# Down projection of a gated ConvFFN: eight of eleven pairs of K tiles as seven products of quarters, with the weights' sums added up in DRAM

## The chip, the cores and the metric

The kernel runs on one core of one Trainium2 chip. The metric is the device time in microseconds (us) of one execution. The engines are TensorE (PE: matmuls; PEld: its weight loads), VectorE (DVE), ScalarE (ACT), GpSimd (POOL) and SyncE (SP), which here only issues DMAs. Each engine works through its own queue in order and waits on semaphores; DMA transfers run on 16 DMA engines that all queues share.

## The reference

One layer of a decoder with 512 positions and a width of 1024: a norm, one wide input projection, a short convolution branch, a gated delta rule branch, a merge, an output projection, and then the part that the change touches:

```python
def conv_ffn(h, w_up, conv_w, w_down):
    up = causal_dwconv(h @ w_up, conv_w)
    gate, val = jnp.split(up, [D_FF], axis=-1)      # D_FF = 2816
    return (jax.nn.silu(gate) * val) @ w_down       # (512, 2816) @ (2816, 1024)

x = x + conv_ffn(rmsnorm(x, norm_ffn_g), w_up, ffn_conv_w, w_down)
return rmsnorm(x, norm_final_g)
```

All of it is in float32, with inputs in float32.

## The kernel before

**Matmuls.** Every large product is done in three matmuls: each operand is split into a high part and the rest (names `wh`, `wl` for weights, `as`, `ts`, `us`, `h` for activations), and low x high, high x low and high x high are added in PSUM. All these matmuls come from one helper, `mm` (L107 before, L108 after). PSUM has 8 banks of 128x512, which `bank()` hands out in turn.

**Jobs.** The program is a list of jobs. A job is a block of weights of 1 MB (four quarters of 128x512, tile `raw`, two buffers) and a function that multiplies with it. `run_jobs` walks the list: it finishes the splitting of this job's block, queues the splitting of the next one, issues the load of the block two jobs on (SP queue), and then emits the job's matmuls. Splitting a quarter is one ACT cast (`wh`, L139 before, L140 after) and one DVE subtraction (`wl`, L140 before, L141 after); twelve `wh` and twelve `wl` quarters are held, three jobs of four.

**What is emitted between matmuls.** `mm` counts columns, and after every 2048 of them calls `tick`, which advances queues of small tasks (splits, evacuations of PSUM, chains of the delta rule) by a step. This, and a scheduler that follows the program's order and its own estimates, sets the order in each engine's queue.

**Projections already in seven products.** Most blocks of the input and up projections already use seven products of quarters instead of eight (`sum_job`): DVE adds weight quarters in SBUF, in `raw` (L160 before), ahead of the split, and 128x256 matmuls follow.

**The down projection.** 2816 rows of `w_down` are 22 K tiles, 11 pairs (11 jobs, from `row_jobs`). The activation is the stationary operand and the weight the moving one. Per pair, `part(g, t)` does, for each of the 4 tiles of 128 positions, 2 halves of the output width and 2 K tiles, three matmuls of 128x512: 48 per pair, 528 in all, into 8 PSUM banks that accumulate over all 11 pairs. `split_ffn` (ACT L298, DVE L299) splits the activation of two K tiles per job. The last two jobs are interleaved by position tiles, so that `fin2(t)` (residual add, final norm, store: DVE L1253 and on, one POOL power L1259, DMAs) starts as soon as tile t is done.

**POOL** has work in the delta rule, four small powers after the output projection (`fin1`, L1142) and four at the end (`fin2`, L1259), and issues no DMA.

Of the kernel before, what the change touches and what calls it, by code (L numbers as in the profile page):

```python
# [9 lines left out]
F32 = mybir.dt.float32  # L10
# [6 lines left out]
P = 128  # L17
# [42 lines left out]
def layer_kernel(ctx, tc, x, norm_mix_g, w_in, w_ab, conv_a_w, gdn_conv_w, gdn_A_log, gdn_dt_bias,  # L60
# [18 lines left out]
    def bank():  # L79
        return ps.tile([P, 512], F32, tag="ps", name=nm("ps"))  # L80


    chains, mids, backs, evacs, splits, sums_of = (deque() for _ in range(6))
    nmm = [0]

    def advance(queue, n):
        while n and queue:
            queue[0].step()
            if queue[0].done:
                queue.popleft()  # L90
            else:
                n -= 1

    def tick():
        advance(backs, 1)
        advance(mids, 1)
        advance(chains, 1)
        advance(evacs, 2)
        advance(splits, 1)
        advance(sums_of, 1)  # L100

    def drain(queue):
        while queue:
            advance(queue, 1)
# [19 lines left out]
    class Block:  # L124
        def __init__(self, src, quarter=(4, P)):
            self.src, self.quarter = src, quarter
            self.raw, self.ready = None, False
# [24 lines left out]
    class SumBlock(Block):  # L152
        def split(self):
# [25 lines left out]
            self.part("12", r[1])  # L179
            yield  # L180

    def run_jobs(jobs):
        jobs[1][0].load()
        for i, (block, use) in enumerate(jobs):
            Task(block.split()).finish()
            drain(splits)
            if i + 1 < len(jobs):
                splits.append(Task(jobs[i + 1][0].split()))
            if i + 2 < len(jobs):
                jobs[i + 2][0].load()  # L190
            use(block.wh, block.wl)


# [20 lines left out]
    def activation_sums(x_, ts, xf):  # L214


        for k in range(0, ND, 2):
            dve.tensor_tensor(out=xf[:, k:k + 2], in0=x_[0][:, k:k + 2].bitcast(F32),
                              in1=x_[1][:, k:k + 2].bitcast(F32), op=ALU.add)
            yield  # L220
            yield
        b = [[xf[:, K * 4:K * 4 + 4, T * HS:T * HS + HS] for T in range(2)] for K in range(2)]

        def to(i, dst, a, c):
            dve.tensor_tensor(out=dst, in0=a, in1=c, op=ALU.subtract)
            yield
            act.copy(out=ts[0][:, i], in_=dst)
# [715 lines left out]
    st = {}  # L943
    held = {}

    def open_conv():
# [172 lines left out]
    def open_o():  # L1119
        drain(evacs)  # L1120
        p1.close()
        fp = ctx.enter_context(tc.tile_pool(name="fp", bufs=1))
        st["x1"] = fp.tile([P, NT, D], F32, name="x1")
        st["h2"] = [fp.tile([P, ND, S], F32R, name=f"h2{i}") for i in range(2)]
# [66 lines left out]
    def split_ffn(k):  # L1191
        if "as" not in st:
            st["as"] = [st["up"].tile([P, 8, S], F32R, tag=f"t{i}", name=f"as{i}") for i in range(2)]
        split(st["as"], k % 8, ffn(k))

    def gate_c(g):
        def c(j, o):
            m = 2 * g + j
            t = st["cvp"].tile([P, S], F32, tag="g", bufs=4, name=nm("g"))
            yield from conv(t, o, ff_w(m), 3)  # L1200
            act.activation(out=t, in_=t, func=AF.Silu)
            gates[m] = t
            yield
        return c
# [29 lines left out]
        sums_of.append(Task(activation_sums(h2, st["ts"], xf)))  # L1234

    for g in range(NF // 2):
        def up_job(i, c, plain):
            if plain:
                return col_job(w_up, i, lambda: st["h2"], c)
            return sum_job(w_up, i, lambda: st["h2"], hsums, c, pair_out)  # L1240

        gj = up_job(g, gate_c(g), g < 2 or g == NF // 2 - 1)
        vj = up_job(NF // 2 + g, val_c(g), True)
        jobs += [(gj[0], first_gate), (vj[0], first_val)] if g == 0 else [gj, vj]

    def fin2(t, acc):
        cvp, x1 = st["cvp"], st["x1"]
# [14 lines left out]
        for sl in halves:  # L1262
            nc.sync.dma_start(out=out2[t * P:(t + 1) * P, sl], in_=y[:, sl])

    def ahead(g):
        for kk in range(2):
            split_ffn(2 * g + kk)
            yield

    def open_down():  # L1270
        drain(evacs)
        Task(ahead(0)).finish()

    def down_x(g):
        return [e[:, 2 * g % 8:2 * g % 8 + 2] for e in st["as"]]
# [56 lines left out]
```

## Time and profile before

| | |
|---|---|
| time, median of 3 runs | 985.68 us (985.62 to 985.8) |
| the profiled execution's own time | 985.69 us |
| its span, first to last instruction | 984.0 us |
| granted TensorE clock, mean | 0.999 |
| PE busy | 974.1 us (99%) |
| DVE busy | 678.8 us (69%) |
| ACT busy | 470.0 us (48%) |
| POOL busy | 60.2 us (6%) |
| DMA | 97.71 MB, 99 GB/s over the span |

Times in the views are from the span's start. "Busy" of PE is the time in which any matmul is under way; matmuls overlap, so their own durations (0.39 us) are longer than the distance from one to the next, and it is the distance that counts. The profile names tiles by the program's names with the numbers left out.

### The profile page before, as it was taken

The page shows a single profiled execution, that of the slowest core. Times are in us where ns is not written, and L with a number is a line of the kernel's source. Part 1 is how long each engine was busy: PE and PEld are TensorE (multiplying, and loading weights), DVE is VectorE, ACT ScalarE, POOL GpSimd, SP SyncE. Part 2 cuts the span into 40 slices and gives each one's busy share as a digit, 9 for nine tenths or more (in the row PEclk, how much of TensorE's full clock was granted, in tenths as well). Part 3 has the DMA queues.
Part 4 walks back from the last instruction along what each step waited for, and adds up shares of the span by engine and source line. Part 5 has one row for each costly group of instructions (what it writes and reads, how often), then busy time and mean ns, then how long its engine had stood idle before and what let it go on. Part 6 is the DMA issues. An engine that isn't in the chain of part 4 may idle for free.

```text
span 984.0 us, 15795 instructions
## 1 busy us (share of the span) xinstructions
PE 974.1 (99%) x6250; PEld 842.3 (86%) x6250; DVE 678.8 (69%) x1312; ACT 470.0 (48%) x1023; POOL 60.2 (6%) x101
## 2 busy tenths in 40 slices
PE   8999999999999999999999999999999999999997
PEld 6888887888888889999988888988999888888885
DVE  6868686896626868899744543998888888533315
ACT  7686566575344434354732323464545556322313
POOL 3320300302000000000000000000000000000000
PEclk9999999999999999999999999999999999999999
DMA  6434212231312123222532252313332234232202
GB/s 228 163 120 128 83 52 87 73 94 53 94 45 86 44 95 120 87 87 87 171 121 94 86 196 82 109 43 129 98 117 86 86 100 158 86 127 88 86 1 85
DMA packets 33466, 97.71 MB, mean 99 GB/s; under 512 B 19275, under 2 KB 19696, under 8 KB 23024
## 3 DMA queue, kind: packets, MB, share of 16 engines
q1 hardware_dynamic: 33392, 96.70, 29.6%
q8 instruction: 49, 0.80, 0.3%
q14 instruction: 25, 0.20, 0.1%
HBM read 93.27 MB, written 3.42 MB: 98 GB/s over the span
## 4 chain that ended last, share of the span: by engine, by line
PE 94%; ACT 3%; DVE 1%; issue 1%; DMA 0%; POOL 0%; SPq 0%; POOLq 0%
PE ps L107 86%; PE ps L609 1%; PE ps L644 1%; PE ps L818 1%; PE ps L838 1%; PE ps L827 0%; ACT Dm L526 0%; PE ps L806 0%; PE ps L805 0%; PE ps L782 0%; PE ps L776 0%; DMA xt<-in_x_dram 0%; PE ps L1154 0%; ACT wh L139 0%; PE ps L720 0%
## 5 line engine op out<-in xcount | busy, mean ns | idle before, releaser
L139 ACT CAST wh<-raw 128x512 fp32r<-128x512 f32 x378 | 222.5, 619 | 287.2 <-PE ps L107 246.9
L140 DVE TENSOR_TENSOR wl<-raw,wh 128x512 fp32r<-128x512 f32 x378 | 253.5, 690 | 144.9 <-ACT wh L139 143.5
L107 PE MATMUL ps<-hT,wh 128*128 128x512 f32 (+1 forms) x1104 | 317.0, 368 | 0.0
L107 PEld LDWEIGHTS ps<-hT,wh 128*128 128x128 f32 x1104 | 196.3, 189 | 28.4
L107 PE MATMUL ps<-hT,wl 128*128 128x512 f32 (+1 forms) x552 | 194.7, 362 | 0.1
L107 PE MATMUL ps<-h,wh 128*128 128x512 f32 (+1 forms) x704 | 177.9, 341 | 0.0
L107 PEld LDWEIGHTS ps<-h,wh 128*128 128x128 f32 x704 | 122.5, 189 | 15.1
L107 PEld LDWEIGHTS ps<-hT,wl 128*128 128x128 f32 x552 | 104.4, 189 | 14.4 <-DVE wl L140 0.5
L107 PE MATMUL ps<-h,wl 128*128 128x512 f32 (+1 forms) x352 | 114.6, 341 | 0.0
L107 PE MATMUL ps<-wh,as 128*128 128x512 f32 x352 | 108.6, 389 | 0.0
L107 PEld LDWEIGHTS ps<-wh,as 128*128 128x128 f32 x352 | 66.1, 188 | 13.7
L107 PEld LDWEIGHTS ps<-h,wl 128*128 128x128 f32 x352 | 66.7, 190 | 7.6
L107 PE MATMUL ps<-wl,as 128*128 128x512 f32 x176 | 68.5, 389 | 0.0
L107 PE MATMUL ps<-ts,wh 128*128 128x256 f32 x320 | 59.2, 283 | 0.0
L305 DVE SCALAR_TENSOR_TENSOR cv<-ps,wA,cv 128x511 f32<-128x511 f32 (+2 forms) x72 | 53.2, 740 | 4.7 <-ACT cv L302 4.5
L107 PEld LDWEIGHTS ps<-ts,wh 128*128 128x128 f32 x320 | 50.6, 192 | 0.0
L160 DVE TENSOR_TENSOR raw<-raw 128x512 f32<-128x512 f32 x72 | 49.3, 685 | 0.9
L107 PE MATMUL ps<-us,wh 128*128 128x256 f32 x256 | 47.4, 283 | 0.0
L107 PEld LDWEIGHTS ps<-us,wh 128*128 128x128 f32 x256 | 40.5, 192 | 0.0
L107 PE MATMUL ps<-wh,mix 128*128 128x512 f32 x128 | 40.2, 391 | 0.0
L107 PE MATMUL ps<-ts,wl 128*128 128x256 f32 x160 | 40.1, 283 | 0.0
L107 PE MATMUL ps<-yas,wh 128*128 128x512 f32 x128 | 39.6, 389 | 0.0
(260 smaller groups left out, 1297.9 us busy)
## 6 DMA issues: line engine op xcount, KB each, us to landing
raw<-in_w_in_dram SPq DMA_DIRECT2D x36, 1024.0 KB, 5.0
raw<-in_w_up_dram SPq DMA_DIRECT2D x22, 1024.0 KB, 4.9
raw<-in_w_down_dram SPq DMA_DIRECT2D x11, 1024.0 KB, 4.9
raw<-in_w_a_out_dram SPq DMA_DIRECT2D x4, 1024.0 KB, 5.0
raw<-in_w_b_out_dram SPq DMA_DIRECT2D x4, 1024.0 KB, 4.9
raw<-in_w_o_dram SPq DMA_DIRECT2D x4, 1024.0 KB, 5.0
Dm<-gtd SPq DMA_DIRECT2D x4, 512.0 KB, 3.9
x<-in_x_dram SPq DMA_DIRECT2D x4, 512.0 KB, 6.7
```

Source lines behind the costliest of these rows:

```text
L107: pe.matmul(o, lhsT=a, rhs=b, start=start, stop=stop, skip_group_check=free)
L139: act.copy(out=wh, in_=src)
L140: dve.tensor_tensor(out=wl, in0=src, in1=wh.bitcast(F32), op=ALU.subtract)
L160: dve.tensor_tensor(out=r[q], in0=a, in1=b, op=op)
L305: dve.scalar_tensor_tensor(out=dst[:, sh:], in0=src[:, :S - sh], scalar=wcol(j), in1=dst[:, sh:], op0=ALU.mult, op1=ALU.add)
L609: pe.transpose(out=o[:, n * P:(n + 1) * P], in_=src[:, n * P:(n + 1) * P], identity=ident)
L644: pe.matmul(o[:, i], lhsT=kqs[:, a, h, 0, sl], rhs=kqs[:, b, h, :, sl], start=a > 0, stop=a + b == 0)
L818: pe.matmul(o[:, 0:P], lhsT=TTf[:, f, :], rhs=rs[h], start=True, stop=True)
L838: pe.matmul(o[:, 0:P], lhsT=A[:, f, :], rhs=vns[h], start=True, stop=True)
```

## The change

Pairs 0, 1, 2, 3, 4, 5, 7 and 8 (`SEVEN`) are done in seven products of quarters; pairs 6, 9 and 10 (`EIGHT`) stay as they were. A quarter of the weight is one K tile by half of the width (W11, W12 of the pair's first K tile, W21, W22 of its second); a quarter of the activation is one K tile by 256 positions.

- **Sums of weights, in DRAM** (`form_down`). For each of the eight pairs four sums are built: V1 = W12 + W11, V3 = W12 + W22, V2 = V1 + W22, V4 = V2 + W21, each as a copy of 256 KB from DRAM to DRAM and an adding transfer of 256 KB on top. These are 64 transfers, 32 of them adding, all issued by POOL. The steps go round the eight pairs, so that an add follows its copy eight or sixteen transfers later. They are emitted from the place where the convolution branch opens (`open_conv`, after the delta rule).
- **Two passes.** Pass A takes the eight pairs with V2, V3, V1 and W11 (24 matmuls each: 4 products, 2 tiles of positions, 3 matmuls) into all 8 banks. Then pair 6 (48 matmuls) starts the output's own banks; at its start `gather` combines the six banks of pass A (2 ACT copies, 8 DVE operations) and adds the results into the residual `x1` (4 DVE operations). Pass B takes the eight pairs again with W21, W22 and V4 (18 matmuls each). Pairs 9 and 10 end it, interleaved by position tiles with `fin2`, as the last two jobs were. The sum is 480 matmuls of 128x512.
- **Sums of activations.** `prep_a` and `prep_b` form them on DVE for two pairs at a time, and `put` splits them (ACT L1302, DVE L1303) into four slots of tile `xs`; `prep_c` splits the plain pairs.
- **Loads.** A pair in pass A loads three sums and one plain quarter (two DMAs, 1 MB together), in pass B two plain quarters and one sum (0.75 MB). From the third down job on the blocks lie in the space of `h2`, the up projection's input (tile `raws`, four blocks), and loads are issued up to four jobs ahead.

```diff
+    SEVEN, EIGHT = (0, 1, 2, 3, 4, 5, 7, 8), (6, 9, 10)
+    down_q = [w_down[g].rearrange("p k (h n) -> p (k h) n", h=2) for g in range(NG)]
+    vsum = {g: dram.tile([P, 4, S], F32, name=f"vs{g}") for g in SEVEN}
+    def form_down():
+        steps = [[(V1, W12, False), (V3, W12, False)], [(V1, W11, True), (V3, W22, True)],
+                 [(V2, None, False)], [(V2, W22, True)], [(V4, None, False)], [(V4, W21, True)]]
+        for step in steps:
+            for g in SEVEN:
+                for to, q, add in step:
+                    src = down_q[g][:, q] if q is not None else vsum[g][:, V1 if to == V2 else V2]
+                    kw = dict(accum_op=ALU.add) if add else {}
+                    tc.keep_in_program_order(pool.dma_start(out=vsum[g][:, to], in_=src, **kw))
+                    yield
+                    yield
...
+        adds.append(Task(form_down()))
...
+    def put(slot, n, i, m, src):
...
+        act.copy(out=xh, in_=src)
+        dve.tensor_tensor(out=xl, in0=src, in1=xh.bitcast(F32), op=ALU.subtract)
+    def prep_a(c):
+        xv, slot = pairs(SEVEN[2 * c], 2), 2 * c % 4
+        d = pair_out().rearrange("p (g t n) -> p g t n", t=2, n=HS)
+        dve.tensor_tensor(out=d, in0=xv[:, :, 0], in1=xv[:, :, :, 1], op=ALU.subtract)
+        dve.tensor_tensor(out=xv[:, :, 0, 1], in0=d[:, :, 1], in1=xv[:, :, 0, 0], op=ALU.subtract)
+        yield
+        put(slot, 2, 0, 2, xv[:, :, 0])
+        yield
+        put(slot, 2, 2, 2, d)
+        yield
+    def times(slot, i, tau, o, wh, wl, start=False, stop=False, free=False):
+        xh, xl = (e[:, slot, i, tau * P:(tau + 1) * P] for e in st["xs"])
+        for k, (a, b) in enumerate(((xl, wh), (xh, wl), (xh, wh))):
+            mm(o, a, b, start and k == 0, stop and k == 2, free)
+    def use_a(p):
+        def use(wh, wl):
...
+            for name, i in (("v2", 1), ("v3", 2), ("v1", 3), ("11", 0)):
+                for tau in range(2):
+                    times(p % 4, i, tau, banks[name][tau], wh[name], wl[name], p == 0, p == N7 - 1)
+    def gather():
...
+            act.copy(out=u, in_=banks["11"][tau])
+            dve.tensor_tensor(out=u, in0=banks["v2"][tau], in1=u, op=ALU.add)
+            dve.tensor_tensor(out=v[:, lo], in0=banks["v3"][tau], in1=u, op=ALU.add)
...
+            dve.tensor_tensor(out=u, in0=o, in1=u, op=ALU.subtract)
+            dve.tensor_tensor(out=v[:, hi], in0=o, in1=v[:, lo], op=ALU.subtract)
...
+            dve.tensor_tensor(out=x1[:, tau, hi], in0=x1[:, tau, hi], in1=us[tau], op=ALU.add)
+            yield
+            dve.tensor_tensor(out=x1[:, tau + 2], in0=x1[:, tau + 2], in1=vs_[tau], op=ALU.add)
...
+    def use_b(p):
...
+            for name, i in (("21", 0), ("22", 2), ("v4", 1)):
+                for tau in range(2):
+                    o = banks["11" if name == "21" else name][tau]
+                    times((p + 2) % 4, i, tau, o, wh[name], wl[name], free=name == "21")
...
-    jobs += row_jobs(w_down, NF, down_x, fin2, open_down, False, lambda g: splits.append(Task(ahead(g + 1))))
+    down = [([(0, 3, vsum[g][:, V2:V1 + 1]), (3, 4, down_q[g][:, W11:W11 + 1])], ("v2", "v3", "v1", "11"), use_a(p))
+            for p, g in enumerate(SEVEN)]
+    eights = [([(0, 4, down_q[g])], range(4), use_c(q)) for q, g in enumerate(EIGHT)]
+    down.append(eights[0])
+    down += [([(0, 2, down_q[g][:, W21:W22 + 1]), (2, 3, vsum[g][:, V4:V4 + 1])], ("21", "22", "v4"), use_b(p))
+             for p, g in enumerate(SEVEN)]
+    down += eights[1:]
+    jobs += [(FormBlock(runs, names, 2 if i < 2 else min(4, i), down_place(i)), use)
+             for i, (runs, names, use) in enumerate(down)]
```

The order of instructions on SP, POOL, ACT, DVE and PE is the same as before up to the last jobs of the up projection, but for POOL's new transfers. Three places differ in a way that matters below.

On POOL, behind the last power of the delta rule (`fac`), before:

```order
L849 TENSOR_TENSOR fac_3256<-fac_3256,nhalf 128x8
L742 COPY TTf<-TT_3435 32x8x32 x4
L849 TENSOR_TENSOR fac_3766<-fac_3766,nhalf 128x8
L1142 TENSOR_TENSOR r_6527<-r_6527,nhalf 128x1
L1142 TENSOR_TENSOR r_6574<-r_6574,nhalf 128x1
```

and now, with each row's waits (`vs` are the sums in DRAM):

```order
L765 COPY TTf<-TT_3443 32x8x32 x3
L872 TENSOR_TENSOR fac_3774<-fac_3774,nhalf 128x8 [waits DVE_49,Pool_49]
L987 DMA vs_368<-in_w_down_dram 128x512 x2
L987 DMA vs_369<-in_w_down_dram 128x512 x2
L987 DMA vs_370<-in_w_down_dram 128x512 x2
L987 DMA vs_371<-in_w_down_dram 128x512 x2
L987 DMA vs_372<-in_w_down_dram 128x512 [waits DMASW0_49]
L987 DMA vs_372<-in_w_down_dram 128x512 [waits DMASW1_49]
```

All 64 issues stand between the last `fac` and the first power of `fin1`; the first eight wait for nothing, and each later one waits for the transfer eight places ahead of it. No other engine's progress is among their waits.

On PE, at the end of pass A (`ps_9125`, `ps_9126` are the two banks of the product with W11, `ps_9501` a bank taken over from V2's product, `raws`-fed `wh_9449` and on are pair 6):

```order
L108 MATMUL ps_9126<-wh_9427,xs_8991 128x512
L108 MATMUL ps_9125<-wh_9449,xs_8992 128x512
L108 MATMUL ps_9125<-wl_9450,xs_8991 128x512
L108 MATMUL ps_9125<-wh_9449,xs_8991 128x512
L108 MATMUL ps_9125<-wh_9465,xs_8992 128x512
L108 MATMUL ps_9125<-wl_9466,xs_8991 128x512
L108 MATMUL ps_9125<-wh_9465,xs_8991 128x512
L108 MATMUL ps_9501<-wh_9457,xs_8992 128x512
```

Pair 6's first matmul adds to a bank that ACT has to copy out first (`gather`); six matmuls later PE needs a bank that DVE has to have read.

The copies stand here in ACT's queue:

```order
L140 CAST wh_9598<-raws_9106 128x512
L140 CAST wh_9617<-raws_9106 128x512
L1360 COPY u_9487<-ps_9125 128x512
L1360 COPY u_9492<-ps_9126 128x512
L1302 CAST xs_8991<-aTa 128x2x512
```

and the last of the operations behind them in DVE's:

```order
L1366 TENSOR_TENSOR u_9492<-ps_9124,u_9492 128x512
L1367 TENSOR_TENSOR o_9493<-ps_9124,o_9493 128x512
L1371 TENSOR_TENSOR x_6375<-x_6375,u_9487 128x512
L1373 TENSOR_TENSOR x_6375<-x_6375,o_9488 128x1024
L1371 TENSOR_TENSOR x_6375<-x_6375,u_9492 128x512
L1373 TENSOR_TENSOR x_6375<-x_6375,o_9493 128x1024
L1303 TENSOR_TENSOR xs_8992<-aTa,xs_8991 128x2x512
```

where before there were only splits:

```order
L140 TENSOR_TENSOR wl_9329<-raw_9252,wh_9328 128x512
L140 TENSOR_TENSOR wl_9337<-raw_9252,wh_9336 128x512
L140 TENSOR_TENSOR wl_9345<-raw_9252,wh_9344 128x512
L299 TENSOR_TENSOR as_9031<-aTa,as_9030 128x512
L140 TENSOR_TENSOR wl_9353<-raw_9252,wh_9352 128x512
L299 TENSOR_TENSOR as_9031<-aTa,as_9030 128x512
```

The last row of the change's piece (`xs` from `aTa`) prepares the activation that pass B's first job multiplies with; it stands behind all twelve operations of `gather`.

More of the change, by code (lines that the diff above doesn't have):

```diff
@@ L80, in bank @@
         return ps.tile([P, 512], F32, tag="ps", name=nm("ps"))
-    chains, mids, backs, evacs, splits, sums_of = (deque() for _ in range(6))
+    chains, mids, backs, evacs, splits, sums_of, adds = (deque() for _ in range(7))
     nmm = [0]
@@ L100, in tick @@
         advance(sums_of, 1)
+        advance(adds, 1)
     def drain(queue):
@@ L126, in __init__ @@
             self.src, self.quarter = src, quarter
-            self.raw, self.ready = None, False
+            self.raw, self.ready, self.lead = None, False, 2
             self.wh, self.wl = {}, {}
@@ L180, in split, with __init__, load @@
             yield
+    class FormBlock(Block):
+        def __init__(self, runs, names, lead, place):
+            super().__init__(None, (S,))
+            self.runs, self.names, self.lead, self.place = runs, names, lead, place
+        def load(self):
+            if self.raw is not None:
+                return
+            self.raw = self.place()
+            for lo, hi, src in self.runs:
+                nc.sync.dma_start(out=self.raw[:, lo:hi], in_=src)
+        def split(self):
+            if self.ready:
+                return
+            self.ready = True
+            for q, name in enumerate(self.names):
+                self.part(name, self.raw[:, q])
+                yield
     def run_jobs(jobs):
@@ L188, in run_jobs @@
                 splits.append(Task(jobs[i + 1][0].split()))
-            if i + 2 < len(jobs):
-                jobs[i + 2][0].load()
+            for j, (later, _) in enumerate(jobs[i + 2:i + 5]):
+                if later.lead >= j + 2:
+                    later.load()
             use(block.wh, block.wl)
@@ L1123, in open_o @@
         st["x1"] = fp.tile([P, NT, D], F32, name="x1")
-        st["h2"] = [fp.tile([P, ND, S], F32R, name=f"h2{i}") for i in range(2)]
+        st["fp"] = fp
+        st["h2"] = [fp.tile([P, ND, S], F32R, tag=f"h2{i}", name=f"h2{i}") for i in range(2)]
         s7 = st["s7"] = p7.enter_context(tc.tile_pool(name="s7", bufs=2))
@@ L1188, in ffn @@
         return st["aT"][1][:, m - NA, :]
[L1191 to L1194, printed above, removed]
     def gate_c(g):
@@ new lines, in use_a @@
+    def use_a(p):
+        def use(wh, wl):
+            if p == 0:
+                drain(evacs)
+                for name in ("v2", "v3", "v1", "11"):
+                    banks[name] = [bank() for _ in range(2)]
+            if p % 2 == 0:
+                splits.append(Task(prep_a(p // 2 + 1) if p < N7 - 2 else prep_c(0)))
+            for name, i in (("v2", 1), ("v3", 2), ("v1", 3), ("11", 0)):
+                for tau in range(2):
+                    times(p % 4, i, tau, banks[name][tau], wh[name], wl[name], p == 0, p == N7 - 1)
+        return use
@@ new lines, in eight, with use_c, use @@
+    def eight(q, t, wh, wl, first=False, last=False):
+        o = banks["out"][t]
+        for hf in range(2):
+            for k in range(2):
+                free = o[hf] in banks["11"]
+                times((0, 2, 3)[q], 2 * k + t // 2, t % 2, o[hf], wh[2 * k + hf], wl[2 * k + hf],
+                      first and k == 0 and not free, last and k == 1, free)
+    kept = []
+    def use_c(q):
+        def use(wh, wl):
+            kept.append((wh, wl))
+            if q == 0:
+                t_ = Task(gather())
+                t_.step()
+                evacs.append(t_)
+                banks["22"], banks["v4"], banks["r"] = ([bank() for _ in range(2)] for _ in range(3))
+                banks["out"] = ([[banks["11"][e], banks["22"][e]] for e in range(2)] +
+                                [[banks["v4"][e], banks["r"][e]] for e in range(2)])
+                splits.append(Task(prep_b(0)))
+                for t in range(NT):
+                    eight(0, t, wh, wl, True)
+            elif q == 1:
+                eight(1, 0, wh, wl)
+            else:
+                for t in range(NT):
+                    if t:
+                        eight(1, t, *kept[1])
+                    eight(2, t, wh, wl, False, True)
+                    fin2(t, banks["out"][t])
+        return use
@@ L1263, in fin2, with down_place, p @@
             nc.sync.dma_start(out=out2[t * P:(t + 1) * P, sl], in_=y[:, sl])
[L1265 to L1275, printed above, removed]
-    jobs += row_jobs(w_down, NF, down_x, fin2, open_down, False, lambda g: splits.append(Task(ahead(g + 1))))
+    def down_place(i):
+        def p():
+            if i < 2:
+                return wp.tile([P, 4, S], F32, tag="raw", bufs=2, name=nm("raw"))
+            if "raws" not in st:
+                st["raws"] = [st["fp"].tile([P, 2, 4, S], F32, tag=f"h2{e}", name=f"raws{e}") for e in range(2)]
+            e = (i - 2) % 4
+            return st["raws"][e // 2][:, e % 2]
+        return p
+    down = [([(0, 3, vsum[g][:, V2:V1 + 1]), (3, 4, down_q[g][:, W11:W11 + 1])], ("v2", "v3", "v1", "11"), use_a(p))
[7 more added lines that the diff above has]
+             for i, (runs, names, use) in enumerate(down)]
     run_jobs(jobs)
```

51 lines of the change are left out of this document (48 added, 3 removed).

## The prediction

> **What bounds the kernel now.** I read the page first: its busy shares, then its chain of waits.
>
> ```profile
> PE 974.1 (99%) x6250; PEld 842.3 (86%) x6250; DVE 678.8 (69%) x1312; ACT 470.0 (48%) x1023; POOL 60.2 (6%) x101
> ...
> PE 94%; ACT 3%; DVE 1%; issue 1%; DMA 0%; POOL 0%; SPq 0%; POOLq 0%
> ```
>
> PE bounds it, so matmuls removed are time removed, as long as PE goes on finding its operands. The view of the split activation (`as`) gives the down projection's extent, and PE's timeline its pace:
>
> ```profile
> L107 PE MATMUL ps<-wh,as x352: 388/389/389, 857.7 to 977.1; 128*128 128x512 f32 x176
> ...
> L107 PE MATMUL ps<-wl,as x176: 389/389/389, 857.9 to 976.9; 128*128 128x512 f32 x176
> ```
>
> ```profile
> 865.63 0.62 PE L107 MATMUL ps<-wh,as 128*128 128x512 f32 x2
> 866.08 0.39 PE L107 MATMUL ps<-wl,as 128*128 128x512 f32 x1
> 866.31 0.62 PE L107 MATMUL ps<-wh,as 128*128 128x512 f32 x2
> ```
>
> 352 + 176 = 528 matmuls start between 857.7 and 977.1: 119.4 / 527 = 0.2266 us from one to the next, and three take 866.31 - 865.63 = 0.68 in the middle too. So there is no gap to win back; only the number of matmuls counts. The windows show the clock and what stands idle beside it:
>
> ```profile
> 820.00:840.00 20.00, 20.00 (x110) 17.43 (x109) 19.04 (x31) 12.69 (x24) 0.00 (x0) 1.00 0.35 116
> 840.00:860.00 20.00, 20.00 (x90) 16.55 (x89) 10.42 (x17) 8.13 (x14) 0.00 (x0) 1.00 0.26 99
> 860.00:880.00 20.00, 20.00 (x90) 16.57 (x89) 6.99 (x12) 5.70 (x10) 0.00 (x0) 1.00 0.30 106
> ```
>
> From left: span, PE, PEld, DVE, ACT, POOL, clock, DMA share, GB/s. At 860 DVE works 7.0 of 20 us and ACT 5.7; ahead of it, at the end of the up projection, DVE has 19.0 of 20.
>
> **Term 1: PE.** A pair had 48 matmuls and has 24 + 18 = 42; eight pairs make 48 fewer, 480 instead of 528. They have the same shape and the same order of operands (low x high, high x low, high x high), so the same distance: 48 x 0.2266 = **10.9 us**.
> The Trainium skill ("TensorE: Matmul & The Clock Gate", section "Back-to-back issue gap") gives about 131 ns as the sustained distance at 512 columns. By that the change would save 48 x 0.131 = 6.3 us; the rows above show 226.6 ns, so the trace disagrees, and I use the trace.
>
> **Term 2: DVE and ACT in the new passes.** Prices, from the groups by shape:
>
> ```profile
> L139 ACT CAST wh<-raw 128x512 fp32r<-128x512 f32 x378 | 222.5, 619 | 287.2 <-PE ps L107 246.9 <-DVE raw L160 36.3 <-DMA raw<-in_w_in_dram 1.3
> L227 ACT CAST ts<-xf 128x1024 fp32r<-128x1024 f32 x4 | 4.2, 1050 | 5.7 <-issue 3.2 <-DVE xf L225 2.5
> L968 ACT COPY o<-ps 128x512 f32<-128x512 f32 x2 | 1.2, 584 | 2.4 <-PE ps L107 2.4
> L140 DVE TENSOR_TENSOR wl<-raw,wh 128x512 fp32r<-128x512 f32 x378 | 253.5, 690 | 144.9 <-ACT wh L139 143.5
> L225 DVE TENSOR_TENSOR xf<-xf 128x1024 f32<-128x1024 f32 x8 | 9.7, 1215 | 0.0
> L1253 DVE TENSOR_TENSOR x<-x,ps 128x512 f32<-128x512 f32 x8 | 5.5, 687 | 17.4 <-PE ps L107 17.4
> ```
>
> Two jobs of pass A are 48 matmuls, 10.9 us. DVE has 8 `wl` (8 x 0.69 = 5.5) and one `prep_a` (three operations on 1024 elements, one on 512: 3 x 1.215 + 0.69 = 4.3): 9.8 us. ACT has 8 x 0.62 + 2 x 1.05 = 7.1. Two jobs of pass B are 36 matmuls, 8.2 us; DVE has 6 x 0.69 + 0.69 + 1.215 + 0.69 = 6.7, ACT 6 x 0.62 + 1.05 + 0.62 = 5.4. So DVE goes from a third to 90% in pass A, but stays below PE, and PE's `wl` are made a job or more ahead: no loss. Beyond that stands part of the `prep_a` work (the subtractions) in the up projection's last jobs, where DVE has these gaps:
>
> ```profile
> 839.04 0.69 DVE L1211 TENSOR_TENSOR aTb<-v,g 128x512 f32<-128x512 f32 x1
> 841.78 0.69 DVE L140 TENSOR_TENSOR wl<-raw,wh 128x512 fp32r<-128x512 f32 x1 [2.04 <-ACT wh L139]
> ...
> 847.22 0.69 DVE L140 TENSOR_TENSOR wl<-raw,wh 128x512 fp32r<-128x512 f32 x1 [2.83 <-ACT wh L139]
> ```
>
> Up to 840 DVE gets six operations on 1024 elements and two on 512 (8.7 us) where eight of 0.69 for `as` stood (5.5): 3.2 us more, which the gaps of 2.0 and 2.8 us take. The down projection still begins at 857.7.
>
> **Term 3: the seam behind pass A.** Pass A ends 192 x 0.2266 = 43.5 us after 857.7, at 901.2. Pair 6's first matmul waits for ACT's copy of the bank with W11. Three matmuls (0.68 us) follow that bank's last; a matmul's result is out 0.39 - 0.23 = 0.16 us after the next begins, and the copy takes 0.58: 0.74 against 0.68, and a signal each way. I take **0.3 us**; the bounds are nothing, and 0.7 if ACT is a cast late. Six matmuls on (1.4 us) PE needs a bank that DVE reads 0.69 after the copy: in time. Behind it DVE has eight operations on PSUM (8 x 0.69), two adds on 512 and two on 1024 (3.8), then the `xs` operation (1.2) for pass B: 10.5 us from the copy's end, against pair 6's 48 matmuls, 10.9, which start about then. Half a microsecond is spare: nothing lost, but this is the tightest place.
>
> **Term 4: loads.**
>
> ```profile
> GB/s 74 422 29 0 0 41 315 176 0 0 0 168 356 0 0 0 66 348 111 0 8 0 225 299 0 0 0 66 406 53 0 0 4 295 238 0 0 0 0 0
> ...
> raw<-in_w_down_dram SPq DMA_DIRECT2D x7, 1024.0 KB, 4.9
> ```
>
> That is 860 to 940 in slices of 2 us: 1 MB flows in about 3 us, lands 4.9 us after its issue, and then the queue rests. Pass A asks for 1 MB per 5.4 us, pass B for 0.75 MB per 4.1: twice as much as before, a little over half of what is shown. The third block can start only when the up projection has read `h2` for the last time, at 857.7; with 0.75 MB of another block ahead of it in SP's queue that is 1.75 MB at 3 us each and 2 us to land, 865; ACT and DVE split its four quarters by 868.2, and its job begins 10.9 us after 857.7, at 868.6, and needs the last quarter 4 us later. In time.
>
> **Term 5: POOL's 64 transfers.** POOL's timeline has room for them:
>
> ```profile
> 307.69 1.64 POOL L849 TENSOR_TENSOR fac<-fac,nhalf 128x8 f32<-128x8 f32 x1 [28.49 <-DVE fac L848]
> 608.30 0.55 POOL L1142 TENSOR_TENSOR r<-r,nhalf 128x1 f32<-128x1 f32 x1 [298.97 <-DVE r L1141]
> ```
>
> They wait only for each other, so they run in one burst from 309.3. Behind them in POOL's queue stands `fin1`'s power, at 608.3: 298.97 / 64 = 4.67 us each are free, and the first sum is loaded past 820. No row shows a transfer within DRAM or an adding one. The lower bound is 256 KB at the 422 GB/s above, 0.6 us (40 us in all), the upper the 4.9 us of a whole MB, and eight are in flight. I take 1 to 2 us each. Their bytes also pass the loads of 309 to 430 on the same DMA engines; ACT waited for a load 1.3 us in the whole input projection, so a load that takes 8 instead of 5 us is mostly covered. **0**, with 1 us as the upper bound.
>
> **The sum.** 984.0 - 10.9 + 0.3 = 973.4 us of span. The profiled execution took 985.69 with a span of 984.0, 1.7 us around it, and the median is 985.68, so nothing is to be corrected: 973.4 + 1.7 = **975.1 us**. PE had no gap in this stage, so below 985.7 - 10.9 = 974.8 there is nothing to gain but the measurement's own spread.
>
> **Rivals.**
>
> *DVE becomes the bound in pass A.* Were its operations on the strided slots of `xs` and on 256-element pieces a fifth longer, two jobs would take 11.8 us against PE's 10.9: 4 x 0.9 = 3.5 us, 978.6. From 11% on it decides. Against it: the same kind of operation on 1024 elements has 1.215 us in all its rows. A miss at the seam (DVE late for pass B) has this size too.
>
> *POOL's issues hold up DVE: slower.* DVE does get slower beside POOL:
>
> ```profile
> 56.45 1.27 DVE L140 TENSOR_TENSOR wl<-raw,wh 128x512 fp32r<-128x512 f32 x1 [1.89 <-ACT wh L139]
> 56.09 1.09 POOL L518 TENSOR_SCALAR_AFFINE_SELECT Dm<-Dm 128x1024 f32<-128x1024 f32 x1
> ...
> sum 123.00, PE 123.00 PEld 110.92 DVE 96.28 ACT 48.12 POOL 1.64; mean PE 20.50 PEld 18.49 DVE 16.05 ACT 8.02 POOL 0.27
> ```
>
> A `wl` of 0.69 us took 1.27, until POOL's operation was over. The last row is 307 to 430 us, where the transfers run: DVE has 123 - 96.3 = 26.7 us free. If each issue held DVE for over 26.7 / 64 = 0.42 us, DVE would be the bound; from 0.58 us the gain is gone; with POOL's 1.09 us it is 64 x 1.09 - 26.7 = 43 us lost, 1018. Against it: an issue moves no tile through POOL.
> The Trainium skill ("SBUF — State Buffer", section "SBUF: two separate sides") describes this port shared by DVE and GpSimd as an exclusive lock, and says that descriptors of GpSimd's DMAs are written through it; no run here shows yet what an issue holds.
>
> *The transfers are slow.* Over 4.67 us each, `fin1` waits for POOL: at the 6.7 us that 512 KB of `x` take to land, 64 x 6.7 - 299 = 130 us, about 1105. With eight in flight this needs 37 us for one.
>
> *The change does not do what it says*: the distance between matmuls grows as their number falls, 985.7. PE's rows give no reason.
>
> **How the numbers follow.** Forecast 975.1: 0.76. DVE-bound passes (978.6): 0.09. The skill's distance (979.7): 0.02. POOL against DVE: 0.08, of it 0.01 still faster, 0.04 even, 0.03 slower. Slow transfers: 0.03. No effect: 0.02. A measurement here tells 0.2% (2 us) from no change: faster 0.76 + 0.09 + 0.02 + 0.01 = 0.88, same 0.04 + 0.02 = 0.06, slower 0.03 + 0.03 = 0.06. The range takes in the first three: from 974.8 less a little spread, 974.4, to 979.7 and the upper bounds of the seam, 980.5.
>
> **What would show it.** Right: `xs` matmuls from 857.7 to about 966.5, 0.2266 apart; one idle time of PE below 0.7 us near 901; POOL's transfers over well before 608; `wl` still 0.69 us between 309 and 430; the tail behind the last matmul still 6.9 us. Wrong: gaps of PE at each pair of jobs in 857 to 901 (DVE), `wl` over 1 us beside POOL's issues, or `ps` matmuls waiting past 912 for `xs`.

## The result and the profile after

| | before | changed |
|---|---|---|
| time, median | 985.74 us of 4 runs (985.62 to 986.17) | 976.32 us of 4 runs (975.77 to 977.62) |
| ratio, 95% interval | | 0.9906, 0.9888 to 0.9923 |
| profiled execution: time, span | 985.69, 984.0 us | 975.77, 973.7 us |
| spans of its runs | 983.5 to 984.3 us (the 15 beside the first four experiments) | 973.7, 974.0, 974.5, 975.5 us |
| time around the span | 1.68 to 1.76 us (the same 15) | 2.02 to 2.12 us |

The change takes 9.4 us off; 10.6 were forecast. The profiled execution is the fastest of its four.

The head of the page after and its chain of waits:

```profile
PE 963.9 (99%) x6202; PEld 833.4 (86%) x6202; DVE 717.8 (74%) x1360; ACT 490.9 (50%) x1049; POOL 104.1 (11%) x165
...
PE 94%; ACT 2%; DVE 1%; DMA 1%; issue 1%; SPq 0%; POOL 0%; POOLq 0%; ACTq 0%
```

PE has 48 matmuls fewer (6250 to 6202) and still bounds the kernel. The view of the split activation `xs` (durations in ns, first and last start in us):

```profile
L108 PE MATMUL ps<-wh,xs x320: 387/389/504, 857.7 to 966.6; 128*128 128x512 f32 x160
L108 PE MATMUL ps<-wl,xs x160: 389/389/402, 857.9 to 966.4; 128*128 128x512 f32 x160
```

480 matmuls start between 857.7 and 966.6, where 528 did up to 977.1. The last start is 10.5 us earlier: 48 x 0.2266 = 10.9, less 0.3 to 0.4 at the seam. The timeline of PE's weight loads shows that wait, for ACT's copy of a bank with W11:

```profile
901.38 0.19 PEld L108 LDWEIGHTS ps<-wh,xs 128*128 128x128 f32 x1 [0.42 <-ACT u L1360]
```

The windows of the new passes (span, PE, PEld, DVE, ACT, POOL, clock, DMA share, GB/s):

```profile
840.00:860.00 20.00, 20.00 (x90) 16.54 (x89) 16.30 (x23) 7.03 (x11) 0.00 (x0) 1.00 0.15 51
860.00:880.00 20.00, 20.00 (x90) 16.57 (x89) 15.44 (x24) 13.49 (x23) 0.00 (x0) 1.00 0.95 341
880.00:900.00 20.00, 20.00 (x90) 16.57 (x89) 13.99 (x22) 11.53 (x19) 0.00 (x0) 1.00 0.56 176
```

At 860 DVE works 15.4 of 20 us where it worked 7.0, and PE stays full. The windows of POOL's burst, after:

```profile
330.00:350.00 20.00, 20.00 (x90) 16.53 (x90) 13.90 (x20) 7.12 (x12) 7.39 (x9) 1.00 0.93 190
350.00:370.00 20.00, 20.00 (x129) 18.30 (x128) 12.81 (x21) 6.95 (x13) 6.78 (x10) 1.00 1.02 209
390.00:410.00 20.00, 20.00 (x126) 18.11 (x126) 16.00 (x27) 7.85 (x15) 8.20 (x13) 1.00 1.04 278
```

and two of the same before:

```profile
330.00:350.00 20.00, 20.00 (x90) 16.54 (x89) 13.92 (x20) 7.13 (x12) 0.00 (x0) 1.00 0.26 94
350.00:370.00 20.00, 20.00 (x129) 18.30 (x128) 12.80 (x21) 6.95 (x13) 0.00 (x0) 1.00 0.28 94
```

PE and DVE do in them what they did before. What changed is the DMA share: 0.26 to 0.93 and more. The 16 engines are full at 190 to 278 GB/s, loads included, though at 860 loads alone reach 341 GB/s at 0.95. The first issue and the last of the 64, and the power of `fin1` behind them, on POOL's timeline:

```profile
309.29 2.90 POOL L987 DMA_DIRECT2D vs<-in_w_down_dram  x5
...
417.21 0.82 POOL L987 DMA_DIRECT2D vs<-in_w_down_dram  x1 [1.67 <-issue]
608.32 0.57 POOL L1189 TENSOR_TENSOR r<-r,nhalf 128x1 f32<-128x1 f32 x1 [190.29 <-DVE r L1188]
```

So the 64 issues stand within 109 us, 1.7 us each, and POOL then rests for 190 us.

The profiled execution thus does what the sum said. Left to explain are the other runs, up to 1.8 us longer, and 0.35 us more around the span.

### The profile page after: what moved, and what is told of

Its sections match the earlier page's. It is cut to its first block, busy times and chain, and to the rows that moved or that the text cites. A ratio compares the mean times of both kernels' runs of the same rounds, so it can differ in the third digit from the quotient of the medians.

```text
span 973.7 us, 15945 instructions
## 1 busy us (share of the span) xinstructions
PE 963.9 (99%) x6202; PEld 833.4 (86%) x6202; DVE 717.8 (74%) x1360; ACT 490.9 (50%) x1049; POOL 104.1 (11%) x165
## 4 chain that ended last, share of the span: by engine, by line
PE 94%; ACT 2%; DVE 1%; DMA 1%; issue 1%; SPq 0%; POOL 0%; POOLq 0%; ACTq 0%
PE ps L108 86%; PE ps L632 1%; PE ps L667 1%; DMA xt<-in_x_dram 1%; PE ps L841 1%; PE ps L861 1%; PE ps L850 0%; ACT Dm L549 0%; PE ps L829 0%; PE ps L828 0%; PE ps L805 0%; PE ps L799 0%; PE ps L1201 0%; PE ps L743 0%; PE ps L752 0%
## 5 line engine op out<-in xcount | busy, mean ns | idle before, releaser
L140 ACT CAST wh<-raw 128x512 fp32r<-128x512 f32 x342 | 199.9, 618 | 219.3 <-PE ps L108 177.4
L141 DVE TENSOR_TENSOR wl<-raw,wh 128x512 fp32r<-128x512 f32 x342 | 228.7, 690 | 80.3 <-ACT wh L140 79.1
L108 PE MATMUL ps<-wh,xs 128*128 128x512 f32 x320 | 99.0, 389 | 0.0
L108 PEld LDWEIGHTS ps<-wh,xs 128*128 128x128 f32 x320 | 60.1, 188 | 12.9 <-ACT u L1360 0.4
L108 PE MATMUL ps<-wl,xs 128*128 128x512 f32 x160 | 62.3, 389 | 0.0
L141 DVE TENSOR_TENSOR wl<-raws,wh 128x512 fp32r<-128x512 f32 x60 | 39.3, 687 | 12.0 <-ACT wh L140 11.6
L140 ACT CAST wh<-raws 128x512 fp32r<-128x512 f32 x60 | 35.7, 620 | 23.3 <-DVE wl L141 8.9
L987 POOL DMA_DIRECT2D vs<-in_w_down_dram x48 | 35.1, 736 | 56.6 <-issue 56.3
```

The costliest lines, as they stand in the source:

```text
L108: pe.matmul(o, lhsT=a, rhs=b, start=start, stop=stop, skip_group_check=free)
L140: act.copy(out=wh, in_=src)
L141: dve.tensor_tensor(out=wl, in0=src, in1=wh.bitcast(F32), op=ALU.subtract)
L987: tc.keep_in_program_order(pool.dma_start(out=vsum[g][:, to], in_=src, **kw))
```

## The experiments

Theory: the gain is 48 matmuls, and all else is covered. Rivals for what is missing: the transfers make loads late by chance; the passes or their loads do it; the transfers' queue costs time around the span (the part of a run's time ahead of the first and behind the last instruction). Every run stands beside runs of the kernel before on the same chip (median 985.42 to 985.64 us).

### The change again, and each half of it alone

The transfers alone, on the kernel before (e1): `form_down`, its queue and its start are added and the sums never read. The passes alone (e2):

```diff
-        adds.append(Task(form_down()))
-    down = [([(0, 3, vsum[g][:, V2:V1 + 1]), ...
+    down = [([(0, 3, down_q[g][:, W12:W22 + 1]), ...
-    ... (2, 3, vsum[g][:, V4:V4 + 1])], ("21", "22", "v4"), use_b(p))
+    ... (2, 3, down_q[g][:, W12:W12 + 1])], ("21", "22", "v4"), use_b(p))
```

> The changed kernel once more, beside the others of this set. Theory (48 matmuls at 0.2266 us fewer, everything else hidden): 975.8 to 976.5 us, span 973.4 to 974.5, 2.0 to 2.1 us around the span. Rival (the sums' transfers disturb the loads of 309 to 430 us by chance): spans scatter over 2 us as in the first four runs, 973.7 to 975.5.

> The kernel before, with the 64 transfers of the sums issued by POOL at the same place; the sums are never read, and the down projection is as before. Theory (hidden in the span, 0.4 us around it): span 984.0, time 986.1 us, ratio 1.0004. Rival (the burst fills the DMA engines and makes loads late): span 984.8 to 985.8, time 987 to 988 us, with more scatter than before.

> The changed kernel without the 64 transfers: the two passes load plain quarters where they loaded sums, as many bytes in the same pieces, so the output is not the reference's. Theory: span 973.4 to 973.7, 1.7 us around it, 975.1 to 975.4 us, and runs within 0.3 us of each other. Rival (the passes, or their loads, are what scatters): 976 to 977 us, with the same scatter as the changed kernel.

| | median (range), us | ratio, 95% interval | spans | around the span |
|---|---|---|---|---|
| change again | 976.15 (975.96 to 976.37) | 0.9905, 0.9892 to 0.9919 | 973.9 to 974.3 | 2.06 to 2.10 |
| transfers alone | 985.94 (985.35 to 986.76) | 1.0005, 0.9996 to 1.0014 | 983.6 to 985.1 | 1.66 to 1.75 |
| passes alone | 975.48 (975.18 to 975.58) | 0.9898, 0.9884 to 0.9911 | 973.1 to 973.5 | 2.08 |

The passes alone come to 975.5, 0.7 us below the change. The transfers alone cost 0.5 us in the median (their interval still holds 1) and scatter over 1.4 us, where the kernel before has 0.9. The profile of the change run again shows how; ACT's and PE's timelines where the burst makes one load late:

```profile
386.94 0.37 ACT L299 COPY o<-ps 128x256 f32<-128x256 f32 x1 [0.82 <-DVE wl L141]
391.27 1.14 ACT L140 CAST wh<-raw 128x512 fp32r<-128x512 f32 x2 [3.96 <-DMA raw<-in_w_in_dram]
...
395.78 0.39 PE L108 MATMUL ps<-hT,wh 128*128 128x256 f32 x1 [0.25 <-DVE u L283]
```

and ACT at the same place without transfers (e2):

```profile
386.87 0.37 ACT L299 COPY o<-ps 128x256 f32<-128x256 f32 x1 [0.82 <-DVE wl L141]
387.21 0.62 ACT L140 CAST wh<-raw 128x512 fp32r<-128x512 f32 x1
```

A cast that starts at 387.2 when the load is in time starts at 391.3; its sums on DVE and its product on PE follow late. Matched one by one, PE's starts of the two profiles drift apart by 0.51 us at 395 and nowhere else between 300 and 970. In the first profile of the change the same load had its cast at 389.0 and PE lost nothing: each run draws another lateness. Over the burst a load of 1 MB lands 6.5 to 8.9 us after its issue, where it took 4.8 to 5.1 before. Theory and rival are both right in part: covered in the luckiest run, 0.5 to 0.7 us in the median.

The queue as the cause of the time around the span falls: with the transfers alone it is 1.7 as before, and without them 2.1 as in the change.

### The seam (e5)

```diff
-            for name, i in (("v2", 1), ("v3", 2), ("v1", 3), ("11", 0)):
+            order = (("v2", 1), ("v3", 2), ("v1", 3), ("11", 0))
+            for name, i in order if p < N7 - 1 else order[-1:] + order[:-1]:
```

> The last pair of pass A multiplies with W11 first and with the three sums after it, so that ACT's copies of the two banks with W11 lie beside 18 matmuls. Theory: PE's wait of 0.4 us near 901 us goes, 0.4 us less than the changed kernel, about 975.9 us beside its 976.3. Rival (the wait moves on to the next bank, which DVE has to have read): PE waits as long at the ninth matmul of pair 6, and the time is that of the changed kernel.

Measured: 975.43 us (975.34 to 975.75), ratio 0.9898 (0.9885 to 0.9912), spans 973.5 to 973.9. ACT's timeline has the copies now at

```profile
896.96 1.27 ACT L1361 COPY u<-ps 128x512 f32<-128x512 f32 x2
```

where they stood at 901.28 in the change's profile of the same set, and PE goes over the seam without a wait. Between these two profiles PE's starts drift by 0.33 us there. They drift by 0.51 at 395 too, since the late load above is in time in e5's profile, so the 0.4 us between the runs' spans may be in part chance. The rest of the 0.7 us in the median is around the span (1.81 to 1.85 for 2.06 to 2.10), for a cause that I did not find: both programs have the same matmuls, in another order only in the last pair of pass A. So the seam cost 0.33 us, near the 0.4 expected, and can be had.

### How near DVE is to being the bound (e6)

```diff
+        for _ in range(2 * (c > 0)):      # 4 in the second kernel
+            dve.tensor_tensor(out=d, in0=xv[:, :, 0], in1=xv[:, :, :, 1], op=ALU.subtract)
```

> Two more DVE subtractions on 1024 elements (2 x 1.22 = 2.4 us) in each of the three prep_a that run in pass A. By the prediction's account of two jobs (9.8 + 2.4 = 12.2 us of DVE against PE's 10.9) DVE becomes the bound: 3 x 1.3 = 3.9 us more than the changed kernel, 980.1. Rival (what counts is DVE's free time over the whole pass, 11 of 43.5 us in the trace, because splits run jobs ahead): 7.3 us more of work fit, no change, 976.2 us.

> Four more such subtractions in each of the three prep_a, 14.6 us in all. By the account of two jobs: 3 x (14.7 - 10.9) = 11.4 us more, 987.6. By the pass as a whole: 14.6 - 11 = 3.6 us more, 979.8 us.

Measured: 975.03 us (974.80 to 976.68) and 975.26 us (975.15 to 975.56): no loss with either. (Their medians are below the change's because the time around the span is 1.7 us here; their spans, 973.1 to 975.0 and 973.4 to 973.9, are like the change's.) The windows with four more operations:

```profile
840.00:860.00 20.00, 20.00 (x90) 16.57 (x89) 20.00 (x25) 8.19 (x12) 0.00 (x0) 1.00 0.14 50
860.00:880.00 20.00, 20.00 (x90) 16.57 (x89) 18.98 (x27) 12.77 (x22) 0.00 (x0) 1.00 0.92 336
880.00:900.00 20.00, 20.00 (x90) 16.57 (x89) 19.05 (x29) 12.24 (x20) 0.00 (x0) 1.00 0.58 179
```

DVE has 58 of 60 us here, 45.7 in the change, and PE is still full. My account of two jobs is refuted, and the account of the pass too, which stopped at its 43.5 us: the splits run ahead, so the idle time of 840 to 860 counts as well. 14.6 us of added work cost nothing, where my account had put the limit at 1.1 us for two jobs. At how much DVE becomes the bound was not reached; the 2 us that it has left in these windows would put it at some 16 us, an estimate.

### Three times the transfers, alone (e1x3)

> The kernel before with the 64 transfers three times over, 192 of them, never read. Theory (POOL is free up to the first power of fin1 at 608 us; a transfer takes 1.7 us in the burst): the burst ends at 309 + 192 x 1.7 = 636 us, fin1 starts 28 us late, and as PE has little to do until h2 is there, the time is about 1010 to 1014 us. Rival (PE has other work to cover, or issues come faster): within 3 us of the kernel before.

```diff
-        for step in steps:
+        for step in steps * 3:
```

Measured: 986.87 us (985.29 to 987.95), ratio 1.0009 (0.9999 to 1.0019), 1.3 us over before. The theory's 1010 fell, for a reason in the order: with 192 transfers to emit, the program reaches `fin1` first, and its powers stand among the issues in POOL's queue, not behind them. So it is no test of a blocked power. It is one of the load: the burst lasts to 684 us, 1.95 us each, and PE's waits between 300 and 860 us are

```profile
PE ps L108 <- DVE u L261: 1.4, 2, 0.7
```

(total, times, longest), two late loads of the kind above. Three bursts cost 1.3 us in the median where one cost 0.5; by their intervals neither is clear of no change, and it is the profile's two waits that show the cause. What a blocked power of `fin1` would cost stays untested.

### Spreading the transfers (e4), and addresses (e7 to e10)

To hold POOL back, it copies one element of the coming job's `wh` ahead of every three issues:

```diff
-        advance(adds, 1)                          # in tick()
+            if adds:                              # in run_jobs, ahead of use()
+                a_ = next(iter(block.wh.values()))
+                tok = const.tile([1, 1], F32, tag="tok", bufs=1, name=nm("tok"))
+                pool.tensor_copy(out=tok, in_=(a_[0:1, 0, 0:1] if len(a_.shape) == 3 else a_[0:1, 0:1]).bitcast(F32))
+                advance(adds, 3)
```

> The change of e5 (W11 first in the last pair), and the transfers in threes: ahead of each job of weights POOL copies one element of that job's first wh, which holds its queue until ACT has split it, and issues three transfers, over some 22 jobs, 309 to about 540 us. Theory (the burst makes a load late by chance, about 0.5 us in the median, and scatters the runs): with 3 transfers per 10 us the loads land in time again, spans 972.9 to 973.3 in all runs, 0.4 to 0.7 us less than e5, 974.8 to 975.2 us. Rival (any transfer beside a load delays it): as e5, 975.4 us with its scatter, or longer, since more jobs have transfers beside them.

Measured: 978.75 us (978.65 to 978.92), ratio 0.9931 (0.9919 to 0.9944). The spans lie close together (976.8 to 977.1, but e5's did too) and PE has no wait between 300 and 860, but it is 3.3 us over e5. PE's own pace had changed:

```profile
L107 PE MATMUL ps<-wh,xs x320: 388/394/397, 858.2 to 969.9; 128*128 128x512 f32 x160
```

111.7 / 479 = 0.2332 us from one matmul to the next, where e5 has 858.0 to 966.6, 0.2267. The clock is the same (1.00). The new tile takes 4 bytes ahead of the weights' pool, which moves `raw`, `wh`, `wl`, `hT` and `h2` up by 32 bytes in each partition and leaves `ts`, `us`, `yas`, `mix` and `xs` in place. So I asked for the shift alone, the pacing with a tile of 64 bytes, and that with `ts` and `us` moved by 32.

```diff
+        pad = const.tile([1, 1], F32, name="pad")        # e7: e5, and this ahead of the burst
+        pool.memset(pad, 0.0)
-                tok = const.tile([1, 1], ...             # e8: e4, and this
+                tok = const.tile([1, 16], ...
-        st["ts"] = [sc.tile([P, 4, 4, HS], ...           # e9: e8, and this, for us too;
+        t_ = pool_.tile([P, 16 * HS + 16], ...           # yas, mix and xs start at 0 of the longer tile
+        return t_[:, 8:16 * HS + 8].rearrange("p (a b n) -> p a b n", b=4, n=HS)
```

> The kernel of e5 with an unused tile of 4 bytes ahead of the weights' pool, which moves raw, wh, wl, hT and h2 up by 32 bytes in each partition and leaves xs, yas, mix, ts and us where they were; no pacing. In e4 the same tile was there. Theory (the 3.3 us that e4 lost came from addresses, not from its pacing): where 512-wide matmuls take one operand from either group, 0.2266 us become 0.2333 (480 of the down projection, 192 of w_a_out, 192 of w_o: 864 x 0.0067 = 5.8 us), the 256-wide ones gain some 1 to 2 us, 978.5 to 979.5 us in all. Rival (the pacing's copies and transfers slowed PE): as e5, 975.4 us.

> The kernel of e4 with POOL's one-element tile padded to 64 bytes, so that the tiles behind it move by 64 bytes and all stay at 32 beyond a multiple of 64, as in the changed kernel. Theory: PE's distance is 0.2266 us again in all stages, and the paced transfers make no load late: spans 972.9 to 973.5 us within 0.4 us of each other, 0.3 to 0.6 us under e5, 974.8 to 975.2 us. Rival (pacing itself costs): 978 to 979 us, as e4.

> The kernel of e8 with the sums of activations of the input and up projections (ts and us) 32 bytes further on, inside tiles that are 64 bytes longer; everything else keeps its address modulo 64. Theory (a 256-wide matmul whose two operands lie 32 bytes apart modulo 64 takes 0.119 us where it takes 0.120, as e4 showed between 380 and 476 and from 630 to 820): 1.5 to 2 us less than e8, 973.0 to 973.4 us. Rival (e4's gain there came from something else that the shift moved): as e8.

Measured: e7 1043.47 us (1042.42 to 1046.51), ratio 1.0591 (1.0576 to 1.0605); e8 971.83 us (971.50 to 971.98), 0.9859 (0.9845 to 0.9872); e9 977.00 us (976.73 to 977.59), 0.9912 (0.9899 to 0.9926).

e7's time has another cause than the one I meant to test. With the pad's memset the scheduler moved all 64 issues up among POOL's first operations, 1.4 to 109 us. Its timeline, its waits on PE up to 200 us and two windows:

```profile
1.41 0.76 POOL L987 DMA_DIRECT2D vs<-in_w_down_dram  x1 [0.31 <-issue]
...
97.48 0.83 POOL L987 DMA_DIRECT2D vs<-in_w_down_dram  x1 [3.60 <-issue]
98.06 0.61 POOL L591 TENSOR_SCALAR g<-g 128x32 f32<-128x32 f32 x1
```

```profile
PE ps L595 <- POOL g L591: 44.0, 1, 44.0
```

```profile
50.00:75.00 25.00, 4.72 (x21) 3.57 (x19) 14.05 (x22) 10.74 (x19) 11.22 (x20) 0.69 0.98 213
75.00:100.00 25.00, 1.06 (x4) 0.93 (x4) 0.87 (x3) 2.79 (x4) 12.97 (x26) 0.50 0.89 168
```

The gate `g` of the delta rule stands in POOL's queue between issues that each wait for an earlier transfer, and PE waits 44 us for it. The granted clock (the column behind POOL) falls to 0.69 and 0.50 in these windows, in which PE has almost no work. This is the prediction's rival of a POOL queue that holds up others, in a place where POOL has work that PE needs: the same 64 transfers cost 0.5 us at 309 and over 60 at the start (1043.5 beside the 978.8 of e4, whose addresses are the same). The 20 us beyond the one wait were not taken apart.

Its matmuls still answer the question. Those on `xs` start from 922.9 to 1034.7 us, 111.8 / 479 = 0.2334, as in e4, without any pacing: the addresses do it. What I had not expected is that e8 and e9 have paces of their own. Mean distances between neighbours, worked out from the starts in each trace, and the offset of the activation's tile from the start of `wh`, modulo 512 bytes, by the tiles' addresses in the program (high and low part have the same offset except in e9). With `yas` the weight is the stationary operand, with `xs` the activation:

| | `yas`, `xs` with 512 columns: offset, us | `ts`, `us` with 256 columns: offset, us |
|---|---|---|
| before (`as` for `xs`), change, e5 | 256: 0.2267, 0.2267 | 256: 0.1200 |
| e4, e7 | 224: 0.2333, 0.2333 | 224: 0.1183 |
| e8 | 192: 0.2333, 0.2289 | 192: 0.1137 |
| e9 | high part 64, low part 128: 0.2316, 0.2311 | high part 96, low part 160: 0.1180 |

(e9's longer tiles had moved the first by 128 bytes and the second by 64, which the expectation did not count.) So 64 is not the modulus: 256 and 192 are the same by it and differ in pace. Nor is it the weights' own address: the up projection's matmuls on `h2`, whose tile moves together with the weights, keep 0.2271 us at 512 columns and 0.1201 to 0.1205 at 256 in all these kernels. The best of both columns is 256 for the wide ones and 192 for the others:

```diff
-        t_ = pool_.tile([P, 16 * HS + 16], ...           # e10: e9, and this
-        return t_[:, 8:16 * HS + 8]...
+        t_ = pool_.tile([P, 16 * HS + 128], ...
+        return t_[:, 0:16 * HS]...                       # ts, us
+        ...  t_[:, 16:16 * HS + 16]                      # yas, mix, xs
```

> The kernel of e8 with ts and us where they are there (192 bytes beyond a multiple of 512 from the start of wh), and yas, mix and xs 64 bytes further on (256 beyond, as in the kernel before), in tiles that are 512 bytes longer. Theory (PE's distance follows from the offset of its two operands modulo 512 bytes): 256-wide matmuls on ts and us stay at 0.1137 us as in e8, and 512-wide ones on yas, mix and xs come back to 0.2267 (192 x 0.0067 + 183 x 0.0020 + 479 x 0.0022 = 2.7 us less than e8), 969.1 us. Rival (it follows from addresses modulo 1024 or more, or from the absolute address): at least one of the two groups leaves these values, and the time is at or above the 971.8 of e8.

Measured: 969.22 us (968.94 to 969.45), ratio 0.9833 (0.9820 to 0.9847), spans 967.1 to 967.6. The theory's 969.1 holds, though `ts` and `us` lie 1024 bytes (high part) and 512 bytes (low part) ahead of their places in e8. The groups of e8:

```profile
L107 PE MATMUL ps<-yas,wh x128: 394/394/395, 485.9 to 530.4; 128*128 128x512 f32 x128
L107 PE MATMUL ps<-wh,xs x320: 387/390/393, 853.5 to 963.2; 128*128 128x512 f32 x160
```

and of e10, with the row of a window in which the 256-wide ones run:

```profile
L107 PE MATMUL ps<-yas,wh x128: 388/390/390, 485.9 to 529.2; 128*128 128x512 f32 x128
L107 PE MATMUL ps<-wh,xs x320: 388/389/390, 851.9 to 960.5; 128*128 128x512 f32 x160
```

```profile
440.00:450.00 10.00, 10.00 (x88) 10.00 (x88) 9.86 (x17) 3.68 (x8) 1.75 (x4) 1.00 0.26 76
```

The 192 matmuls on `yas` take 43.3 us from first to last start, for 44.5 in e8; those on `xs` 108.6 for 109.7; and in 10 us there are 88 matmuls (36 of them on `hT`, whose pace does not change), where the change has

```profile
440.00:450.00 10.00, 10.00 (x86) 10.00 (x85) 9.91 (x18) 5.62 (x11) 0.00 (x0) 1.00 0.08 11
```

This is the fastest kernel of the study: 7 us below the change, 16.4 below before. What pacing alone saves was not measured apart from the addresses; e9's five runs spread over 0.9 us though its transfers are paced.

## Why the prediction was right, and where it was not

**Term 1, PE: right.** 10.9 us for 48 matmuls; the last start is 10.5 us earlier, the seam's wait taken off. The distance stayed at 0.2267, but for a reason that the prediction did not have: not shape and order of operands alone, but because the new tile `xs` lies where `as` lay, 256 bytes modulo 512 from `wh`. The prediction did not look at addresses, so this part was luck. At 0.2333 (e4) the 480 matmuls would have cost 3.2 us of the gain. The 131 ns of the Trainium skill ("TensorE: Matmul & The Clock Gate", section "Back-to-back issue gap") were rightly set aside: all measured distances at 512 columns are between 0.2267 and 0.2333 us.

**Term 2, DVE in the passes: right that nothing is lost, wrong on the margin.** The step that failed is "9.8 us" of DVE in every 10.9. Only three `prep_a` run in pass A, and the splits and sums run ahead, so the share is 74% (29.4 of 40 us), and the rival's "from 11% on it decides" was far too near: four more operations in each `prep_a`, half as much again, cost nothing.

**Term 3, the seam: right.** 0.3 forecast; the weight load waited 0.42 and PE's starts lost 0.33, in the place and for the reason given; DVE's work behind it was in time.

**Term 4, loads of the passes: right.** ACT's timeline has the first two casts' groups of `raws`:

```profile
863.84 2.19 ACT L140 CAST wh<-raws 128x512 fp32r<-128x512 f32 x4 [5.24 <-DMA raws<-vs]
866.45 2.19 ACT L140 CAST wh<-raws 128x512 fp32r<-128x512 f32 x4 [0.42 <-DMA raws<-vs]
```

The third block landed at 863.8 and was cast by 866.0, forecast 865 and 868.2.

**Term 5, the transfers: right on POOL, too small on the loads.** 1.7 us each, within 1 to 2, and the last issued by 418. But the cost was put at 0 with 1 us as the bound, on the argument that a load of 8 us for 5 is mostly covered. It is mostly: 0 in the profiled run, 0.5 to 0.7 in the median. The 8 us were right (median 8.3), but with the DMA engines full one load lands after 6.5 us and another after 8.9, and the same load was late by another amount in each profile; the argument had no term for that.

**The sum.** It was made for the profiled execution (973.4 of span, 973.7 measured), and the median lies 0.55 above that one. The 1.7 us around the span became 2.07; e1 and e2 show that the transfers are not why, and what is stays open. 10.9 - 0.33 (seam) - 0.35 (around the span) - 0.65 (transfers) = 9.6, measured 9.4.

**POOL against DVE: fell.** The `wl` of the same stretch before, and in the burst after:

```profile
L140 DVE TENSOR_TENSOR wl<-raw,wh x59: 678/684/694, 311.6 to 429.9; 128x512 fp32r<-128x512 f32 x59
L141 DVE TENSOR_TENSOR wl<-raw,wh x59: 678/684/694, 311.6 to 429.9; 128x512 fp32r<-128x512 f32 x59
```

The three durations are the same. An issue occupies POOL for 0.53 to 1.00 us and holds DVE for nothing that shows. The Trainium skill ("SBUF — State Buffer", section "SBUF: two separate sides") has a DVE operation with two inputs in SBUF take the shared port only against a GpSimd operation that reads SBUF. The trace agrees as far as it goes: 1.27 us beside POOL's own arithmetic on `Dm`, no delay beside issues that move data within DRAM.

## What to carry to other kernels

In a kernel that PE bounds, count matmuls, and check that the activation's tile keeps its offset from the weights' tile: moving one by 32 or 64 bytes changed PE's pace by 1 to 5%, in opposite directions for 256 and 512 columns, and putting each at the best offset tried was worth 2.6 us beside e8. A free engine's queue is free only where nothing that the bound engine needs stands in it, and a burst that fills the DMA engines has a cost that a lucky profile does not show: PE waited for it in one profile of the six with one burst from 309 us on, and the median lost 0.5 to 0.7 us. With the transfers in threes PE waited in none of four; whether that saves the whole cost stays open. A share of busy time over one stretch is no decision point where work can run ahead.

## What the runs showed of the hardware that was not expected

- The distance between matmuls depends on where the two operands lie to each other in a partition: 0.2267 to 0.2333 us at 512 columns and 0.1137 to 0.1200 at 256, at the same granted clock. All rows fit an offset modulo 512 bytes; 256 would fit too, and the runs do not tell these apart, nor do they rule out 128. At the same offset of 192, 512-column matmuls took 0.2333 us with the weight stationary and 0.2289 with the activation stationary; why is open.
- With the transfers within DRAM under way the DMA engines are full at 190 to 278 GB/s, while loads into SBUF alone reach 341 at the same share. 256 KB land 7.0 us (copies from `w_down` and adds) or 7.3 us (copies within the sums) after their issue in the median. Plain copies in place of the adds were not tried.
- The time around the span differs between programs with the same work: 1.7 us before, 2.1 in the change, 1.8 with the order of e5, 1.7 with more DVE operations. No run shows why.
